# Layer b's first key and value panels planned as a pair of seven products in a two-layer trunk

## The chip, the cores and the metric

The kernel runs on one core of a Trainium2 chip. The metric is device time in microseconds (us) for one execution of the whole program, which is one launch. Engines are named as in the profile: PE (TensorE, the matmuls), PEld (its weight loads), ACT (ScalarE), DVE (VectorE), POOL (GpSimd) and SP (SyncE, which here only issues DMAs).

## The reference, cut to what matters

256 rows of 2048 numbers pass through a layer a (attention with forget gates, then an MLP with a squared ReLU) and a layer b. Between them one projection makes the keys and values that layer b attends to. All matrices are fp32.

```python
h = h + o.reshape(B, S, D) @ a_w_out[l]                      # layer a
h = h + sq_relu_mlp(h, mlp_norm_g[layer], mlp_w1[layer], mlp_w2[layer])
...
kv = rms_norm(h, kv_norm_g) @ kv_w                           # 2048 -> 4096, the panels of this case
k_sh, v_sh = jnp.split(kv, [D], axis=-1)
k_sh = rms_norm(k_sh.reshape(B, S, H, Dh), kv_k_g)           # per head
...
q = rms_norm((u @ b_w_q[l]).reshape(B, S, H, Dh), b_q_g[l])  # layer b
o = chunked_relbias_attention(q, k_sh, v_sh, b_rel[l])
h = h + o.reshape(B, S, D) @ b_w_out[l]
h = h + sq_relu_mlp(h, mlp_norm_g[layer], mlp_w1[layer], mlp_w2[layer])
```

## The kernel before, in words

**Units.** Every weight matrix is cut into panels of 512 output columns, and a panel into eight units of 128 partitions x 1024 elements: two row tiles of 128 rows each, 512 columns wide. The 256 activation rows make two blocks of 128, so a unit meets four products of 128 x 128 by 128 x 512.

**Three passes.** fp32 values are split in two. `issue` makes a weight unit's upper part with one ACT copy (L318, `hi`) and its lower part with one DVE subtraction (L319, `lo`). `passes` then runs each product three times: activation's upper part by `hi` (L585), its lower part by `hi` (L587), its upper part by `lo` (L589). A plain unit (`products`) is therefore 12 matmuls of 512 columns. Three `hi` and three `lo` buffers exist, so the split of a unit waits until the unit three places earlier has gone through its second pass (`hi`) or third pass (`lo`).

**Pairs.** Two panels that share an activation can be a `Pair`. The first two units of either panel form a 2 x 2 arrangement, `11`, `12`, `21`, `22`, and these four units are multiplied in seven smaller products in place of eight. Here the seven are called F0 to F6: `11`, T3, T2, T1, `21`, T4, `22`. T3, T2, T1 and T4 are sums of units: T3 and T2 are made by DVE (`make`, L951), T1 and T4, in most pairs, by a DMA of POOL that adds to what is there (`put`, L960). F1, F2, F3 and F6 meet sums of activations (`S`, `Sh`), made in the same manner. One such product is 6 matmuls; its results are put together by ACT copies (L985, L989, L995) and DVE operations (L990, L1002). The remaining units of both panels, a2 to a7 and b2 to b7, run plainly. In place of a unit of their own, the first four products of a pair interleave with the last three units, b5 b6 b7, of the pair before.

**Order.** The order on SP, ACT, DVE and PE is the written one. `plan_heads`, `plan_mlp` and `plan_out` write the list of units, `run` walks it. `AHEAD = 2` units are split ahead of use and `EARLY = 3` are loaded ahead of that. Other work (making the split activations `act<-y`, L410 to L414; head norms L653 to L688; attention; the steps of the hidden layer, whose sums of activations are `Sh`, L398) is cut into steps, which `run_fill` places between units. How many steps go behind each unit, and how many units after their start, stands in tables of numbers (`KM`, `HM`, `T0H`, `KX` and others); the tables with six numbers tell how many units ahead of a pair its parts `12`, `22`, `21`, `11`, T3 and T1 are loaded or made. POOL's order is the scheduler's.

**The place of the change.** At the end of layer a's MLP stand four panels of query weights, as two pairs; the last has the order `""` in `plan_mlp`. Then come keys and values: head group 0 has the panels K0 and V0, and groups 1 to 3 their own. Before the change K0 and V0 go through `panels` as plain units (16 units, the last three of V0 joined with the next pair through `Tail`), and only groups 1 to 3 are pairs, of the order `kv`. The relative-position bias is loaded by POOL ahead of each group's attention (`rel_bias`, L1214 and L1216).

Of the kernel before, what the change touches and what calls it, by code (L numbers as in the profile page):

```python
# [15 lines left out]
P = 128  # L16
# [4 lines left out]
H = 16  # L21
# [6 lines left out]
UN = 1024  # L28
AHEAD = 2
TABLES = {  # L30
    "ATA": ((11, 13, 15, 19, 9), (9, 12, 16, 18, 11), (8, 13, 15, 19, 9), (9, 9, 12, 12, 10)),
    "ATB": ((10, 13, 14, 18, 9), (9, 13, 15, 17, 11), (9, 12, 15, 17, 10), (7, 10, 12, 12, 9)),
# [13 lines left out]
    "LONG": ((0, 1, 2, 5, 9, 10, 11, 14, 14), (0, 0, 0, 4, 7, 9), (1, 0, 1, 2, 5, 5), (1, 0, 1, 4, 5, 5)),  # L46
    "OFH": (11, 10, 1, 7, 7, 7),
    "OFK": (10, 9, 4, 9, 8, 4),
# [3 lines left out]
    "OSH": (7, 9, 7, 5, 5, 1),  # L52
    "OSK": (9, 7, 4, 7, 5, 1),
    "OUTH": "F a2 a3 b2 a4 a5 b3 b4 F G F G b5 a6 a7 G b6 b7 G c2 G c3 G d2 c4 c5 G c6 c7 d3 d4",
    "OUTK": "a2 a3 F b2 a4 F b3 a5 F b4 b5 G G a6 a7 G b6 G c2 b7 d2 G c3 G c4 c5 c6 G c7 d3 d4",
    "QF": (4, 4, 2, 3, 2, 1),
    "QS": (10, 4, 4, 8, 3, 1),
    "RI": (3, 5, 7, 5),
    "SHORT": ((4, 0, 0, 3, 6, 8, 8, 9, 12), (2, 2, 3, 3, 7, 7, 8, 10, 13), (2, 0, 0, 2, 6, 7), (0, 0, 0, 2, 4, 5)),
# [39 lines left out]
def trunk(ctx: ExitStack, tc: tile.TileContext, xT, xr, gs, hg, bf, wgate, w_in, w_oa, w1a, w1fa, w1sa, w2fa, w2sa,  # L99
# [94 lines left out]
    def plan_mlp(w1, w1f, w1s, w2f, w2s, rest, when, more=None):  # L194
        pairs = []

        def add(w, wf, ws, i, wides, order, times, cols=WIDE):
            j = wides.index(i) if i in wides else i - sum(1 for k in wides if k < i)
            names = ("11", "12", "21", "22")
            if i in wides:  # L200
                m = 8 - cols // 512
                src = [[None] * (8 - m) + [ws[m * (2 * j + q) + u] for u in range(m)] for q in range(2)]
                big = {k: wf[4 * j + m] for m, k in enumerate(names)}
            else:
                src = [[w[16 * j + 8 * q + u] for u in range(8)] for q in range(2)]
                big = {k: src[int(k[1]) - 1][int(k[0]) - 1] for k in names}
            pairs.append(Pair(big, src, order, len(pairs) % 2 == 1, times, cols if i in wides else UN))

        rooms = {"12": "v0", "22": "k0", "11": "k1", "21": "v1"}
        seq = [(0, 0, 0), (0, 0, 1)]  # L210
        for c in range(NCH):
            seq += [(1, c, 0)] + [(0, c + 1, 0)] * (c + 1 < NCH) + [(1, c, 1)] + [(0, c + 1, 1)] * (c + 1 < NCH)
        for m, (second, c, q) in enumerate(seq):
            i = 2 * c + q
            if second:
                add(None, w2f, w2s, i, WIDE2, "deep%d" % q, TABLES["W2L" if i == 7 else "W2S" if q else "W2F"], DEEP)
            else:
                add(w1, w1f, w1s, i, WIDE1, "ahead%d" % q if i else "early", TABLES["W1E" + when] if not i else TABLES["W1I" + when] if i == 1 else TABLES["W1S" if q else "W1F"], DEEP)
            pairs[-1].at = second, c, q
        if more is not None:  # L220
            for q in range(2):
                add(more, None, None, q, (), "" if q else "query", TABLES["QS" if q else "QF"])
                pairs[-1].at = 1, NCH, q
        plan, rest = join(pairs, rooms, rest)
        return queue(plan + rest)

    def queue(plan):
        units.extend(Form(p, i, q == 3) if q > 1 else p.src[q][i] for p, q, i in plan)
# [28 lines left out]
                plan.append((a if t[0] in "ab" else b, "abcd".index(t[0]) % 2, int(t[1])))  # L257
        return plan, [(b, 1, u) for u in (5, 6, 7)]

    def plan_heads(w, when, w_out):  # L260
        pairs = []
        for j in range(1, w.shape[0] // 16):
            src = [[w[16 * j + 8 * q + u] for u in range(8)] for q in range(2)]
            big = {k: src[int(k[1]) - 1][int(k[0]) - 1] for k in ("11", "12", "21", "22")}
            pairs.append(Pair(big, src, "qkv" if when == "H" else "kv", j % 2 == 1, TABLES[when + ("F" if j == 1 else "S")]))
            pairs[-1].at = 2 * j
        tail = Tail(w, 8)
        units.extend(w[i] for i in range(13))
        plan, rest = join(pairs, {"12": "k0", "22": "k1", "11": "v0", "21": "v1"}, [(tail, 0, u) for u in range(KT // UA - 3, KT // UA)])
# [5 lines left out]
    plan_a = plan_mlp(w1a, w1fa, w1sa, w2fa, w2sa, rest, "H", w_qb)  # L275
    plan_k, rest, tail_k = plan_heads(w_kv, "K", w_ob)
    plan_b = plan_mlp(w1b, w1fb, w1sb, w2fb, w2sb, rest, "K")
    ready = deque()

    raws = deque()  # L280
# [420 lines left out]
    class Rooms:  # L701
# [208 lines left out]
    def bring(p, name):  # L910
# [5 lines left out]
        elif p.order in LAZY:  # L916
# [10 lines left out]
    def make(p, name, half=None):  # L927
# [89 lines left out]
    def mlp(plan, x, Sx, st, last, more=None):  # L1017
# [204 lines left out]
    def heads_b(out):  # L1222
# [135 lines left out]
```

## Time and profile before

| what | value |
|---|---|
| median of 3 runs | 2059.22 us (2059.14 to 2059.76) |
| the profiled execution | 2062.13 us, its span 2060.3 us |
| mean granted TensorE clock | 0.999 |
| PE busy | 2047.3 us, 99% |
| PEld, DVE, ACT, POOL busy | 82%, 86%, 68%, 12% |
| DMA | 556.72 MB, mean 270 GB/s |

The span is the profiled part of the execution; 1.8 us of its time lie around it. Matmuls overlap, and the ends of matmuls are modelled, so starts are read rather than ends. In the windows below the columns are PE, PEld, DVE, ACT, POOL (busy us, instructions in parentheses), granted clock (1.00 is full speed), the mean busy share of the DMA engines and GB/s.

### The profile page before, as it was taken

What the parts mean: (1) busy time and instruction counts of PE and PEld (TensorE: products, weight loads), DVE (VectorE), ACT (ScalarE), POOL (GpSimd) and SP (SyncE); (2) the same over time, 40 slices, a digit from 0 to 9 for tenths busy, and PEclk for the clock granted to TensorE, in tenths of its full rate; (3) what the DMA queues carried; (4) which work ended last, traced back from release to release, by engine and by line L of the source; (5) the groups of instructions that cost most, each with busy time, mean ns of one, the idle gap of its engine ahead of it and who ended that gap; (6) DMA issues with size and microseconds to landing.
All of it is one profiled execution on the core that took longest, in us unless ns stands there. A gap on an engine that the chain in (4) does not pass through costs nothing.

```text
span 2060.3 us, 27092 instructions
## 1 busy us (share of the span) xinstructions
PE 2047.3 (99%) x9068; PEld 1690.6 (82%) x9068; DVE 1778.3 (86%) x2058; ACT 1400.0 (68%) x1799; POOL 238.7 (12%) x347
## 2 busy tenths in 40 slices
PE   9999999999999999999999999999999999999999
PEld 8888888878888888888888888888788887888887
DVE  7788798899898899899987778888988988988996
ACT  7766566677677677677788566666766675776764
POOL 1121010011111102101012111001111111111020
PEclk9999999999999999999999999999999999999999
DMA  8898897898888898898878988889988888888985
GB/s 330 258 301 252 275 278 249 292 274 266 293 255 287 267 295 272 248 290 276 252 247 273 288 265 269 251 256 295 279 288 269 266 267 277 262 285 258 293 263 150
DMA packets 174444, 556.72 MB, mean 270 GB/s; under 512 B 40528, under 2 KB 69088, under 8 KB 151264
## 3 DMA queue, kind: packets, MB, share of 16 engines
q1 hardware_dynamic: 153824, 464.99, 63.9%
q0 software_dynamic: 20192, 89.70, 22.4%
q8 instruction: 71, 1.16, 0.2%
q14 instruction: 69, 0.57, 0.1%
q10 hardware_dynamic: 288, 0.30, 0.1%
HBM read 515.02 MB, written 27.29 MB: 263 GB/s over the span
## 4 chain that ended last, share of the span: by engine, by line
PE 88%; DMA 4%; issue 3%; DVE 3%; ACT 1%; SPq 0%; POOL 0%; ACTq 0%; DVEq 0%; POOLq 0%
PE acc L589 21%; PE acc L585 21%; PE acc L587 21%; PE s L585 8%; PE s L587 8%; PE s L589 8%; DVE lo L319 1%; DMA wT<-in_w1fb 1%; DMA q<-turn 1%; PE po L720 1%; PE po L757 1%; DMA w<-in_w2fb 1%; ACT hi L318 1%; DVE z L433 0%; DMA turn<-z 0%
## 5 line engine op out<-in xcount | busy, mean ns | idle before, releaser
L319 DVE TENSOR_TENSOR lo<-raw,hi 128x1024 fp32r<-128x1024 f32 (+1 forms) x414 | 500.3, 1213 | 81.0 <-ACT hi L318 76.6
L318 ACT ACTIVATE hi<-raw 128x1024 fp32r<-128x1024 f32 (+1 forms) x414 | 435.1, 1055 | 195.2 <-PE acc L587 128.6
L585 PE MATMUL acc<-hi,act 128*128 128x512 f32 x1784 | 500.5, 393 | 4.3 <-ACT hi L318 3.7
L589 PE MATMUL acc<-lo,act 128*128 128x512 f32 x1784 | 493.9, 390 | 0.2
L587 PE MATMUL acc<-hi,act 128*128 128x512 f32 x1784 | 493.8, 390 | 0.1
L585 PEld LDWEIGHTS acc<-hi,act 128*128 128x128 f32 x1784 | 333.1, 188 | 75.3 <-ACT hi L318 6.1
L587 PEld LDWEIGHTS acc<-hi,act 128*128 128x128 f32 x1784 | 335.1, 188 | 71.6 <-DVE act L414 1.0
L589 PEld LDWEIGHTS acc<-lo,act 128*128 128x128 f32 x1784 | 334.5, 188 | 72.4 <-DVE lo L319 3.1
L318 ACT ACTIVATE hi<-w 128x1024 fp32r<-128x1024 f32 x258 | 271.4, 1059 | 125.9 <-PE acc L587 83.5
L319 DVE TENSOR_TENSOR lo<-w,hi 128x1024 fp32r<-128x1024 f32 x258 | 310.6, 1219 | 19.6 <-ACT hi L318 17.7
L319 DVE TENSOR_TENSOR lo<-wT,hi 128x1024 fp32r<-128x1024 f32 x220 | 266.9, 1222 | 68.6 <-ACT hi L318 64.7
L318 ACT ACTIVATE hi<-wT 128x1024 fp32r<-128x1024 f32 x220 | 231.8, 1060 | 103.7 <-PE acc L587 42.2
L585 PE MATMUL s<-hi,act 128*128 128x512 f32 x530 | 146.3, 391 | 0.0
L589 PE MATMUL s<-lo,act 128*128 128x512 f32 x530 | 145.0, 389 | 0.4 <-DVE lo L319 0.4
L587 PE MATMUL s<-hi,act 128*128 128x512 f32 x530 | 144.7, 388 | 0.0
L459 POOL DMA_DIRECT2D q<-z x192 | 95.7, 511 | 250.9 <-DVE z L433 214.4
L589 PEld LDWEIGHTS s<-lo,act 128*128 128x128 f32 x530 | 99.2, 188 | 21.4 <-DVE lo L319 1.1
L587 PEld LDWEIGHTS s<-hi,act 128*128 128x128 f32 x530 | 99.4, 188 | 20.6
L585 PEld LDWEIGHTS s<-hi,act 128*128 128x128 f32 x530 | 99.2, 188 | 20.4
L585 PE MATMUL s<-hi,S 128*128 128x512 f32 x288 | 89.6, 392 | 0.0
L587 PE MATMUL s<-hi,S 128*128 128x512 f32 x288 | 88.7, 389 | 0.0
L589 PE MATMUL s<-lo,S 128*128 128x512 f32 x288 | 88.6, 389 | 0.0
(213 smaller groups left out, 2236.3 us busy)
## 6 DMA issues: line engine op xcount, KB each, us to landing
raw<-in_w_in SPq DMA_DIRECT2D x75, 512.0 KB, 5.8
w<-in_w2fa SPq DMA_DIRECT2D x32, 1024.0 KB, 6.2
w<-in_w2fb SPq DMA_DIRECT2D x32, 1024.0 KB, 6.6
w<-in_w1fa SPq DMA_DIRECT2D x28, 1024.0 KB, 7.4
w<-in_w1fb SPq DMA_DIRECT2D x28, 1024.0 KB, 7.1
raw<-in_w2sa SPq DMA_DIRECT2D x52, 512.0 KB, 7.1
raw<-in_w_kv SPq DMA_DIRECT2D x52, 512.0 KB, 5.4
raw<-in_w2sb SPq DMA_DIRECT2D x51, 512.0 KB, 7.6
```

Of the source, the lines that this page charges most:

```text
L318: S.activation(hi[:, c], raw[:, c], AF.Copy)
L319: V.tensor_tensor(lo[:, c], raw[:, c], hi[:, c].bitcast(F32), op=ALU.subtract)
L459: (G if i % 2 else SY).dma_start(dst[32 * j : 32 * j + 32, i * n : (i + 1) * n], z[32 * i : 32 * i + 32, j * n : (j + 1) * n])
L585: TE.matmul(ps[:, cols], xh, cut(hi, j), start=first, stop=False, **kw)
L587: TE.matmul(ps[:, cols], xl, cut(hi, j), start=False, stop=False, **kw)
L589: TE.matmul(ps[:, cols], xh, cut(lo, j), start=False, stop=last, **kw)
L720: TE.matmul(s[:, P : 3 * P], q[:, a, P:T], k[:, a], start=True, stop=True)
L757: TE.matmul(po[:, :T], v[:, 0, a * P : (a + 1) * P], pT[:, :2], start=True, stop=False)
```

## The change: K0 and V0 as a pair

K0 and V0 become a pair of their own, of the order `kv0`. The first two units of either panel, four plain units in all, are replaced by the seven products. F0 to F3 stand between b4 and b7 of the last query pair. For that, `12`, `22`, `21` and `11` of the new pair are loaded into the lower halves of rooms whose upper halves the last query pair now takes; T3 has a query room. `plan_mlp` hands its last three units on in place of queueing them, and `Rooms.open` takes its tile only when it is first used. The host lays out K0 like the other panels. The tables were written anew; the second W1 pair is named `second`, which has the order of units that it had before as `ahead1`.

```diff
+    "KZ": (7, 8, 3, 7, 5, 3),
-    "T0H": ((0, -1, 6, 6, 7, 7, 7, 10, 11), (1, -1, 5, 7, 7, 7, 8, 9, 9), (1, 4, 6, 6, 7, 7), (0, -1, 4, 4, 4, 5)),
+    "T0H": ((1, -1, 6, 6, 6, 6, 6, 8, 8), (0, -1, 4, 5, 6, 6, 7, 8, 8), (0, 4, 6, 7, 7, 7), (1, -1, 5, 5, 5, 5)),
...
-        return queue(plan + rest)
+        return (queue(plan), rest) if more is not None else (queue(plan + rest), [])
...
-    def plan_heads(w, when, w_out):
+    def plan_heads(w, when, w_out, rest=None):
         pairs = []
-        for j in range(1, w.shape[0] // 16):
+        for j in range(1 if rest is None else 0, w.shape[0] // 16):
...
-            pairs.append(Pair(big, src, "qkv" if when == "H" else "kv", j % 2 == 1, TABLES[when + ("F" if j == 1 else "S")]))
+            order = "qkv" if when == "H" else "kv" if j else "kv0"
+            pairs.append(Pair(big, src, order, j % 2 == 1, TABLES["KZ" if j == 0 else when + ("F" if j == 1 else "S")]))
...
-    plan_k, rest, tail_k = plan_heads(w_kv, "K", w_ob)
+    plan_k, rest, _ = plan_heads(w_kv, "K", w_ob, rest)
...
+        elif p.order == "":
+            p.t[name] = sub(p.rooms[name])[:, :UN]
...
+            elif p.order == "kv0":
+                t[name] = query_room(3)
...
-        run(plan, open_pair)
+        run(plan, open_pair, None, plan_k[0][0] if more else None)
...
-        box = [13]
-
-        def after():
-            prepare(plan_k[0][0], box[0])
-            box[0] -= 1
-
-        panels(xkv, evacs[:1], None, after)
-        panels(xkv, evacs[1:2], None, after, tail=tail_k)
...
-        "w_kv": np.concatenate([_cols_a(kv[:, :1024]), _cols_a(kv[:, 1024:], True)]),
+        "w_kv": _cols_a(kv, True),
```

Line numbers of the changed kernel are higher: L318 becomes L323, L319 L324, L398 L403, L585/L587/L589 become L590/L592/L594, L951 L962, L960 L971, L985 L996, L1214 and L1216 L1225 and L1227. On PE, at the end of the query panels, the order of before runs from the last unit of the last query pair (`s`) to the first unit of K0 (`acc`):

```order
L585 MATMUL s<-hi,act 128x512 x4
L587 MATMUL s<-hi,act 128x512 x4
L589 MATMUL s<-lo,act 128x512 x4
L585 MATMUL acc<-hi,act 128x512 x4
L587 MATMUL acc<-hi,act 128x512 x4
L589 MATMUL acc<-lo,act 128x512 x4
```

and of now, from F0 over b5 to F1, where `S` is the sums of activations:

```order
L590 MATMUL acc<-hi,act 128x512 x2
L592 MATMUL acc<-hi,act 128x512 x2
L594 MATMUL acc<-lo,act 128x512 x2
L590 MATMUL s<-hi,act 128x512 x4
L592 MATMUL s<-hi,act 128x512 x4
L594 MATMUL s<-lo,act 128x512 x4
L590 MATMUL acc<-hi,S 128x512 x2
L592 MATMUL acc<-hi,S 128x512 x2
L594 MATMUL acc<-lo,S 128x512 x2
```

F0 stands three query units earlier than K0's first unit did, and the same interleaving goes on: b6, F2, b7, F3, a2, F4, a3, a4, F5, a5, a6, a7, F6, b2. On ACT the order of now at this place holds the splits of T3 and T2 (`hi<-query`) and the copy `p<-acc`, which reads what F1 left:

```order
L323 ACTIVATE hi<-query 128x1024
L323 ACTIVATE hi<-raw 128x1024
L693 ACTIVATE q<-z,gqk 128x1024
L672 ACTIVATE qn<-acc,ss 128x128 x4
L996 ACTIVATE p_9866<-acc 128x512
L323 ACTIVATE hi<-query 128x1024
L1006 ACTIVATE acc<-acc 128x512
```

Before, the same steps of norms were followed by splits of raw units alone:

```order
L667 ACTIVATE qn<-acc,ss 128x128 x4
L318 ACTIVATE hi<-raw 128x1024
L688 ACTIVATE q<-z,gqk 128x1024
L667 ACTIVATE qn<-acc,ss 128x128 x4
L318 ACTIVATE hi<-raw 128x1024 x3
```

The copy `p<-acc` is new here and stands directly ahead of T2's split. On POOL the order of before, from the first load of the bias `rb` on, is

```order
L1214 DMA rb<-in_rel 128x4x256
L1216 MEMSET rb 64x4x64
L661 TENSOR_TENSOR ss<-ss,mhalf 128x4 x4
L960 DMA R<-in_w_kv 128x1024
L960 DMA wT_10136<-in_w_kv 128x1024
```

and of now

```order
L971 DMA R<-in_w_kv 128x1024
L666 TENSOR_TENSOR ss<-ss,mhalf 128x4 x2
L1225 DMA rb<-in_rel 128x4x256
L1227 MEMSET rb 64x4x64
L971 DMA query<-in_w_kv 128x1024
L666 TENSOR_TENSOR ss<-ss,mhalf 128x4 x2
L971 DMA R<-in_w_kv 128x1024
L971 DMA wT_10086<-in_w_kv 128x1024
```

The new pair's T1 (`R`, first row) and T4 (`query`) came in; T4 stands behind the MEMSET on `rb`. The last place is on DVE at the start of layer a's MLP, where the second set of sums `Sh` of the hidden layer is made. Before:

```order
L319 TENSOR_TENSOR lo<-raw,hi 128x1024
L319 TENSOR_TENSOR lo<-wT_4140,hi 128x1024
L951 TENSOR_TENSOR wT_4140<-wT_4140,w_4074 128x1024
L398 TENSOR_TENSOR Sh<-sum,Sh 128x512 x2
L319 TENSOR_TENSOR lo<-wT_4140,hi 128x1024
L951 TENSOR_TENSOR wT_4140<-wT_4140,w_4074 128x1024
```

and now

```order
L403 TENSOR_TENSOR Sh<-sum,Sh 128x512 x2
L324 TENSOR_TENSOR lo<-raw,hi 128x1024
L324 TENSOR_TENSOR lo<-wT_4144,hi 128x1024
L962 TENSOR_TENSOR wT_4144<-wT_4144,w_4074 128x1024
L324 TENSOR_TENSOR lo<-wT_4144,hi 128x1024
L962 TENSOR_TENSOR wT_4144<-wT_4144,w_4074 128x1024
```

The sums moved from between the two splits of `wT` to ahead of the raw unit's split.

More of the change, by code (lines that the diff above doesn't have):

```diff
@@ L30 @@
 TABLES = {
-    "ATA": ((11, 13, 15, 19, 9), (9, 12, 16, 18, 11), (8, 13, 15, 19, 9), (9, 9, 12, 12, 10)),
-    "ATB": ((10, 13, 14, 18, 9), (9, 13, 15, 17, 11), (9, 12, 15, 17, 10), (7, 10, 12, 12, 9)),
[1 row of a table removed]
+    "ATA": ((10, 13, 15, 19, 9), (9, 12, 15, 18, 12), (8, 13, 15, 19, 9), (9, 9, 12, 12, 10)),
+    "ATB": ((11, 12, 14, 18, 9), (9, 13, 15, 17, 11), (9, 12, 15, 17, 10), (7, 10, 12, 12, 10)),
[1 row of a table added]
     "GS": (1,),
[11 rows of a table removed]
-    "LONG": ((0, 1, 2, 5, 9, 10, 11, 14, 14), (0, 0, 0, 4, 7, 9), (1, 0, 1, 2, 5, 5), (1, 0, 1, 4, 5, 5)),
-    "OFH": (11, 10, 1, 7, 7, 7),
-    "OFK": (10, 9, 4, 9, 8, 4),
[3 rows of a table removed]
-    "OSH": (7, 9, 7, 5, 5, 1),
[12 rows of a table added]
+    "LONG": ((0, 1, 2, 5, 9, 10, 11, 14, 14), (0, 0, 0, 4, 7, 9), (0, 0, 1, 2, 5, 5), (1, 0, 1, 4, 5, 5)),
+    "OFH": (11, 10, 2, 7, 7, 6),
+    "OFK": (9, 9, 4, 8, 8, 4),
[3 rows of a table added]
+    "OSH": (10, 7, 9, 6, 5, 1),
     "OSK": (9, 7, 4, 7, 5, 1),
[L54 to L57, printed above, removed]
+    "OUTH": "F a2 a3 a4 b2 a5 b3 b4 F F G G b5 a6 a7 G b6 b7 G c2 G c3 G d2 c4 c5 c6 G c7 d3 d4",
+    "OUTK": "a2 a3 F b2 a4 F b3 a5 F b4 b5 G G a6 a7 G b6 G c2 b7 G d2 c3 G c4 c5 c6 G c7 d3 d4",
+    "QF": (4, 3, 2, 4, 2, 1),
+    "QS": (10, 4, 4, 8, 4, 2),
     "RI": (3, 5, 7, 5),
-    "SHORT": ((4, 0, 0, 3, 6, 8, 8, 9, 12), (2, 2, 3, 3, 7, 7, 8, 10, 13), (2, 0, 0, 2, 6, 7), (0, 0, 0, 2, 4, 5)),
[1 row of a table removed]
+    "SHORT": ((4, 0, 0, 4, 7, 7, 7, 8, 11), (2, 2, 3, 3, 7, 7, 8, 11, 13), (4, 0, 0, 2, 6, 6), (0, 0, 1, 2, 4, 5)),
[1 row of a table added]
     "T": ((1, -1, 5, 14, 14, 14, 15, 20, 20), (0, 2, 8, 10, 10, 14, 18, 20, 22), (0, -1, 5, 6, 7, 7), (0, -1, 4, 5, 5, 5)),
[4 rows of a table removed]
[4 rows of a table added]
     "W1F": (7, 5, 1, 5, 4, 3),
[2 rows of a table removed]
[2 rows of a table added]
     "W1S": (8, 6, 4, 5, 4, 1),
     "W2F": (6, 5, 1, 5, 4, 3),
[1 row of a table removed]
[1 row of a table added]
     "W2S": (7, 7, 4, 5, 3, 1),
-    "XOH": (9, 12, 13, 11),
-    "XOK": (9, 14, 12, 14),
-    "XS": (0, 5, 6, 2),
+    "XOH": (9, 13, 12, 11),
+    "XOK": (10, 14, 12, 14),
+    "XS": (0, 5, 5, 0),
 }
 EARLY = 3
-LAZY = ("qkv", "kv", "out0", "out1")
+LAZY = ("qkv", "kv", "kv0", "out0", "out1")
 UA = UN // 512
@@ L217, in plan_mlp @@
             else:
-                add(w1, w1f, w1s, i, WIDE1, "ahead%d" % q if i else "early", TABLES["W1E" + when] if not i else TABLES["W1I" + when] if i == 1 else TABLES["W1S" if q else "W1F"], DEEP)
+                add(w1, w1f, w1s, i, WIDE1, ("second" if i == 1 else "ahead%d" % q) if i else "early", TABLES["W1E" + when] if not i else TABLES["W1I" + when] if i == 1 else TABLES["W1S" if q else "W1F"], DEEP)
             pairs[-1].at = second, c, q
@@ L258, in plan_out @@
         return plan, [(b, 1, u) for u in (5, 6, 7)]
-    def plan_heads(w, when, w_out):
+    def plan_heads(w, when, w_out, rest=None):
         pairs = []
-        for j in range(1, w.shape[0] // 16):
+        for j in range(1 if rest is None else 0, w.shape[0] // 16):
             src = [[w[16 * j + 8 * q + u] for u in range(8)] for q in range(2)]
             big = {k: src[int(k[1]) - 1][int(k[0]) - 1] for k in ("11", "12", "21", "22")}
-            pairs.append(Pair(big, src, "qkv" if when == "H" else "kv", j % 2 == 1, TABLES[when + ("F" if j == 1 else "S")]))
+            order = "qkv" if when == "H" else "kv" if j else "kv0"
+            pairs.append(Pair(big, src, order, j % 2 == 1, TABLES["KZ" if j == 0 else when + ("F" if j == 1 else "S")]))
             pairs[-1].at = 2 * j
-        tail = Tail(w, 8)
-        units.extend(w[i] for i in range(13))
-        plan, rest = join(pairs, {"12": "k0", "22": "k1", "11": "v0", "21": "v1"}, [(tail, 0, u) for u in range(KT // UA - 3, KT // UA)])
+        tail = None
+        if rest is None:
+            tail = Tail(w, 8)
+            units.extend(w[i] for i in range(13))
+            rest = [(tail, 0, u) for u in range(KT // UA - 3, KT // UA)]
+        plan, rest = join(pairs, {"12": "k0", "22": "k1", "11": "v0", "21": "v1"}, rest)
         q = pairs[-1].rooms
@@ L274, in trunk @@
     plan_h, rest, tail_h = plan_heads(w_in, "H", w_oa)
-    plan_a = plan_mlp(w1a, w1fa, w1sa, w2fa, w2sa, rest, "H", w_qb)
-    plan_k, rest, tail_k = plan_heads(w_kv, "K", w_ob)
-    plan_b = plan_mlp(w1b, w1fb, w1sb, w2fb, w2sb, rest, "K")
+    plan_a, rest = plan_mlp(w1a, w1fa, w1sa, w2fa, w2sa, rest, "H", w_qb)
+    plan_k, rest, _ = plan_heads(w_kv, "K", w_ob, rest)
+    plan_b, rest = plan_mlp(w1b, w1fb, w1sb, w2fb, w2sb, rest, "K")
     ready = deque()
@@ L705, in open @@
         def open(self):
-            self.t = prob.tile([P, 4 * UN], F32, name="pbuf", tag="p", bufs=1)
+            self.t = None
             self.n = dict.fromkeys(self.at, 0)
         def __call__(self, name):
+            if self.t is None:
+                self.t = prob.tile([P, 4 * UN], F32, name="pbuf", tag="p", bufs=1)
             first, n = self.at[name]
```

44 rows, old and new, of the table TABLES are left out of this document.

## The prediction

> **What bounds the kernel now.** I read the head of the page first, then the windows by stage, then PE's waits and the chain.
>
> ```profile
> span 2060.3 us, 27092 instructions
> PE 2047.3 (99%) x9068; PEld 1690.6 (82%) x9068; DVE 1778.3 (86%) x2058; ACT 1400.0 (68%) x1799; POOL 238.7 (12%) x347
> PE 88%; DMA 4%; issue 3%; DVE 3%; ACT 1%; SPq 0%; POOL 0%; ACTq 0%; DVEq 0%; POOLq 0%
> ```
>
> PE is busy in all but 13.0 us of the span, and 88% of the chain that ended last is PE's own work. So a matmul that goes is worth its full time wherever PE is not waiting, and the rest is decided by what PE waits for. The place of the change is the stretch from 1060 to 1180 us; the other three rows are layer b's W1 start, and two windows of 11 us that stand for the starts of both MLPs.
>
> ```profile
> 1060.00:1180.00 120.00, 120.00 (x535) 99.53 (x533) 92.94 (x112) 87.43 (x139) 20.94 (x17) 1.00 0.87 269
> 1400.00:1480.00 80.00, 78.23 (x336) 63.60 (x335) 71.12 (x80) 56.34 (x67) 10.70 (x19) 0.98 0.92 296
> 455.00:466.00 11.00, 10.59 (x45) 7.93 (x44) 10.93 (x11) 7.34 (x9) 0.30 (x1) 1.00 0.97 327
> 1475.00:1486.00 11.00, 11.00 (x50) 9.10 (x49) 10.93 (x12) 8.02 (x10) 0.10 (x1) 1.00 1.04 357
> PE acc L585 <- ACT hi L318: 3.7, 4, 1.7
> PE acc L585 <- DVE acc L990: 1.9, 1, 1.9
> ```
>
> In the first row PE is busy 120.00 of 120.00 us: there is no wait to take away where K0 and V0 run, only work. The last two rows are PE's largest waits (us in all, times, longest), and neither lies in that stretch.
>
> **The matmuls.** PE's timeline around the last query unit and the first unit of K0:
>
> ```profile
> 1107.31 1.07 PE L585 MATMUL s<-hi,act 128*128 128x512 f32 x4
> 1110.03 1.07 PE L585 MATMUL s<-hi,act 128*128 128x512 f32 x4
> 1115.47 1.07 PE L585 MATMUL s<-hi,act 128*128 128x512 f32 x4
> 1118.19 1.07 PE L585 MATMUL acc<-hi,act 128*128 128x512 f32 x4
> ```
>
> These are first passes of b4, b5 and b7 of the last query pair and of K0's first unit. A unit of 12 matmuls takes 1110.03 - 1107.31 = 2.72 us, so a matmul takes 0.227 us and a product of 6 takes 1.36 us. Four plain units (48 matmuls) become seven products (42). That is 6 x 0.227 = **1.36 us less** on a PE that here never waits.
>
> **What is added on ACT and DVE.** Three more splits, T3 and T2, the combining copies and operations. The rows are groups, those of the stretch 1060 to 1180 first; two of them also give the shares of the stretch from b3 to the ninth unit of K0 and V0, and of one that is as full.
>
> ```profile
> L318 ACT ACTIVATE hi<-raw 128x1024 fp32r<-128x1024 f32 x38 | 40.1, 1063 | 14.1 <-PE acc L587 7.2 <-PE acc L589 1.7 <-DVE ss L656 1.5
> L413 ACT ACTIVATE act<-y 128x1024 fp32r<-128x1024 f32 x4 | 4.2, 1062 | 0.1
> L410 ACT ACTIVATE y<-query,gsb 128x256 f32<-128x256 f32 x8 | 3.6, 504 | 1.6 <-DVE act L414 1.6
> L653 ACT ACTIVATE sq<-acc 128x512 f32<-128x512 f32 x8 | 4.5, 592 | 3.3 <-PE acc L589 3.3
> L667 ACT ACTIVATE qn<-acc,ss 128x128 f32<-128x128 f32 x32 | 9.1, 372 | 1.6 <-POOL ss L661 1.6
> L688 ACT ACTIVATE q<-z,gqk 128x1024 f32<-128x1024 f32 x4 | 4.6, 1159 | 1.4 <-DMA z<-turn 1.4
> L985 ACT ACTIVATE p<-s 128x512 f32<-128x512 f32 x2 | 1.2, 598 | 4.5 <-PE s L589 4.5
> L319 DVE TENSOR_TENSOR lo<-raw,hi 128x1024 fp32r<-128x1024 f32 x37 | 45.0, 1222 | 9.2 <-ACT hi L318 8.8 <-PE acc L587 0.2
> L951 DVE TENSOR_TENSOR query<-query,w 128x1024 f32<-128x1024 f32 x1 | 1.2, 1226 | 0.0
> L990 DVE SCALAR_TENSOR_TENSOR acc<-s,p 128x512 f32<-128x512 f32 x2 | 1.4, 680 | 0.0
> 1085.00:1135.00 50.00, 50.00 (x223) 41.39 (x222) 36.80 (x42) 39.87 (x67) 10.96 (x8) 1.00 0.86 268
> 985.00:1010.00 25.00, 25.00 (x112) 20.71 (x111) 24.29 (x26) 18.58 (x25) 0.87 (x1) 1.00 0.87 232
> ```
>
> ACT gains 3 x 1.063 for splits and 3 x 0.598 for copies, 4.98 us: 39.87 becomes 44.9 of 50. DVE gains 3 x 1.222, 2 x 1.226 and 2 x 0.68, 7.5 us: 36.80 becomes 44.3 of 50. Both still fit, and the last row shows PE at 25.00 of 25.00 with DVE at 24.29 of 25. So none of it costs PE time by its amount; it can cost by its order.
>
> The tightest place in the order is T2's split. Now `p<-acc` stands ahead of it on ACT, and that copy waits until F1 is through. F0 takes b5's old start, 1110.03; b5 follows at 1111.39, F1 at 1114.11 and ends at 1115.47; b6 fills the time to 1118.19, where F2 needs T2's upper part, and its lower part two passes of 0.45 later, at 1119.10. After F1's end come the copy (0.60), the split's upper part (1.06) and its lower part (1.22): 1115.47 + 2.88 = 1118.35, which is 0.75 ahead of the third pass. That holds if ACT is there when F1 ends. Its queue from the split of b4 to the copy can start when the second pass of a7, three units ahead, is through (1107.31 - 3 x 2.72 + 1.81 = 1100.96). It holds five splits, two `act<-y`, six `y`, two squares, eight `qn` and one `q<-z`: 5.32 + 2.12 + 3.02 + 1.18 + 2.98 + 1.16 = 15.78 us, to 1116.7, if durations are added up. Then T2's lower part is there at 1119.6, about 0.5 us late. But starts in the trace follow each other closer than durations. An identical sequence is there for the next pair:
>
> ```profile
> 1159.19 0.60 ACT L985 ACTIVATE p<-s 128x512 f32<-128x512 f32 x1 [3.47 <-PE s L589]
> 1160.77 1.23 DVE L319 TENSOR_TENSOR lo<-wT,hi 128x1024 fp32r<-128x1024 f32 x1 [3.20 <-ACT hi L318]
> 1162.62 0.62 PE L589 MATMUL s<-lo,S 128*128 128x512 f32 x2
> ```
>
> There ACT idled 3.47 us ahead of the copy, the lower part ended at 1162.00, its pass started at 1162.62, and PE did not wait. I take **+0.2 us**, between 0 and 1.0 (twice the sum's lateness, for a DVE that is late too). Below nothing is excluded, since PE has no wait here to lose.
>
> **The sums of the hidden layer in layer a.** The tables also move work elsewhere, mostly by a place or two. One move meets a wait that the trace shows:
>
> ```profile
> 458.82 0.61 PE L585 MATMUL acc<-hi,Sh 128*128 128x512 f32 x2
> 459.44 0.73 PE L587 MATMUL acc<-hi,Sh 128*128 128x512 f32 x2
> 460.58 0.73 PE L589 MATMUL acc<-lo,Sh 128*128 128x512 f32 x2 [0.40 <-DVE lo L319]
> 461.15 1.08 PE L585 MATMUL s<-hi,act 128*128 128x512 f32 x4
> ```
>
> Three passes of 0.45 took 461.15 - 458.82 = 2.33 us in place of 1.36, because `lo` of T2's kind stood on DVE right behind `Sh`. Now `Sh` stands ahead of the raw unit's split, exactly as it stands in layer b, before and after. Layer b's window (1475 to 1486) has PE at 11.00 of 11.00 us. So I take **-0.97 us**; the ends are -0.97 and 0, the latter if another split is late for it.
>
> The other moves of tables I cost at 0, since the same work lies on the same engines a place or two away, under a PE that is busy 99%. The bound is the largest single wait of PE above, 1.9 us, either way.
>
> **The sum.** -1.36 + 0.2 - 0.97 = -2.13. The profiled execution took 2062.13 us (its span 2060.3, and 1.83 around it), so it would take 2060.0. The median of the runs stands 2.91 below the profiled execution; by the same distance the forecast is **2057.1 us**. Against the median that is -0.1%; a measurement of this kernel can tell apart from no change about 0.2%, which is 4.1 us.
>
> **The clock.** One wait of layer b's W1 start costs more than itself:
>
> ```profile
> 1441.43 12.97 DMA wT<-in_w1fb
> 1454.50 1.06 ACT hi L318
> 1455.00:1460.00 5.00, 4.39 (x12) 3.52 (x13) 4.41 (x4) 3.72 (x5) 0.18 (x1) 0.66 0.80 304
> ```
>
> An accumulating DMA landed after 12.97 us, PE waited for the split behind it (the 1.7 us wait for `hi` above), and in the next 5 us the granted clock was 0.66: 5 x 0.34 = 1.7 us lost. So a stall of this size, not its bare length, is the price of a late T4: up to twice as much. The Trainium skill, page "TensorE: Matmul & The Clock Gate", section "Part 1: The HAM clock gate", says that the clock halves after an idle window of about 3.4 us, and that pauses of PE beyond that are to be avoided. By that rule a new wait of under 3.4 us in the new pair would not slow the clock, and the sum's ends would be 1.7 us closer; the trace does not agree, as 1.7 us of waiting were enough here, and I keep the trace's price. In layer b's MLP I leave wait and clock as they are, since POOL's order there is the same.
>
> **The rivals.** *Waits go too.* Thirteen us of PE's span are not busy, and the rewritten tables move parts of pairs in both MLPs. If the late T4 at 1454 lands in time, 1.7 us of waiting and 1.7 us of clock go with it: -2.13 - 3.4 = -5.5, **2053.7 us**. Against it: that DMA's row on POOL is unmoved and the queues are as full. Chance 0.17.
>
> *The new pair eats its gain.* If ACT and DVE queue up from F1 to F6, at most one buffer's lateness of about 1 us at T2 and again behind T1 (each the bound above), the total is about -0.1 to 0: with `Sh` not helping either, **2059.1 us**. For it: 44.9 and 44.3 of 50 us, with waits on both sides. Against it: the full window at 985 us. Chance 0.16.
>
> *T4 is late behind the bias.* This one ends slower. T4 of the new pair is an accumulating DMA, and on POOL it stands behind the MEMSET on `rb`, which waits for the landing of `rb`; PE needs T4 at F5.
>
> ```profile
> 1113.21 0.83 POOL L1214 DMA_DIRECT2D rb<-in_rel  x1 [1.00 <-DVE act L414]
> 1119.28 0.30 POOL L1216 MEMSET rb<- 64x256 f32 x1 [5.24 <-DMA rb<-in_rel]
> DMA to landing us min/median/max: 5.0/5.9/8.2
> DMA to landing us min/median/max: 5.2/9.3/13.0
> ```
>
> The last two rows are the landings of L1214 (the bias) and of L960 (all accumulating DMAs). F5 is due at 1110.03 + 5 x 1.36 + 6 x 2.72 = 1133.15 (five products and six plain units stand ahead), so T4 must have landed by 1132.1, one split earlier. With the issue at 1113.21 and the medians it lands at 1113.21 + 0.83 + 5.9 + 0.30 + 9.3 = 1129.5, in time by 2.6 us. With the longest of both, and 2.4 us of new DVE work ahead of what `rb` waits for (T3's sum and a split, 1.226 + 1.222), it lands at 1138.0, 5.9 us late, and the clock's 1.7 us come on top: -2.13 + 5.9 + 1.7 = +5.5, **2064.7 us**. It decides against the change when T4 lands later than 1132.1 + 0.4, and past the 0.2% when later than about 1136.6. Chance 0.08, since both longest landings must meet.
>
> That the change does not do what it says I leave out: the order shows F0 to F3 among the query units, and 42 matmuls for 48.
>
> **How the numbers follow.** The forecast, 0.59, lies between -3.3 (without the T2 lateness, and with 1.0 us more found by the tables) and about 0, that is 2055.9 to 2059.2. The chances of the rivals are 0.17, 0.16 and 0.08. Faster by over 0.2% (under 2055.1): the first rival, 0.17, and 0.03 of the forecast's tail: 0.20. Slower by over 0.2% (over 2063.3): T4's worst landings, 0.08, of which some end within, and an unseen wait with the halved clock (1.9 + 1.7 on top of a lost gain, about 2062.8): together 0.08. Within: 0.72. The range that leaves 2 in 10 out reaches to the first rival's 2053.7 and above to 2061.5 (the lost gain, 2059.1, with one such wait of 1.9 and a little more).
>
> **What would show it.** Right: PE's timeline has F0 at the place of b5, seven products of 1.36 us, no PE wait between b4 and b2 of the new pair, F5 about 23 us behind F0; the three passes with `Sh` in layer a's MLP start take 1.36 us; ACT's `p<-acc` starts within 1 us of F1's end. Wrong: the accumulating `query<-in_w_kv` lands after F5's time and PE waits on ACT `hi` there; a granted clock below 1.00 in the pair's window; or waits that come or go in windows that this text costs at 0, above all at 1454 us.

## The result, and the profile after

The changed kernel took 2055.78 us (median of 22 runs, 2053.41 to 2059.09) against 2059.63 us before (22 runs beside them, 2056.45 to 2063.48): a ratio of 0.9982, 95% interval 0.9976 to 0.9988. That is 3.8 us faster, just inside the 0.2% that the prediction called no change and inside its range, with nearly double the movement that it forecast (2.1 us). One kernel's runs differ by several us, so sizes below rest on ratios and on traces, not on single times.

The head of the page of the changed kernel, with PE's two largest waits (us, times, longest):

```profile
span 2053.8 us, 27091 instructions
PE 2044.1 (100%) x9062; PEld 1688.7 (82%) x9062; DVE 1784.0 (87%) x2065; ACT 1403.6 (68%) x1805; POOL 244.3 (12%) x349
PE 97%; DVE 2%; ACT 1%; issue 1%; DMA 0%; ACTq 0%; DVEq 0%
PE acc L594 <- DVE lo L324: 2.4, 2, 1.4
PE s L594 <- DVE lo L324: 1.3, 1, 1.3
```

PE's share of the chain rose from 88% to 97%; DMA, 4% before, left it. The waits for ACT's `hi` behind a late DMA and for `acc L990` are gone from the top, and waits for `lo` have come in their place. By stage, the windows that answer to those of before:

```profile
1060.00:1180.00 120.00, 118.71 (x524) 97.48 (x523) 97.63 (x116) 90.88 (x145) 24.41 (x19) 1.00 0.89 275
1105.00:1140.00 35.00, 35.00 (x156) 28.99 (x155) 29.51 (x33) 28.69 (x47) 9.59 (x7) 1.00 0.97 288
1085.00:1135.00 50.00, 50.00 (x222) 41.38 (x222) 43.29 (x50) 43.31 (x72) 14.35 (x10) 1.00 0.98 304
1400.00:1480.00 80.00, 79.93 (x350) 64.91 (x348) 74.04 (x82) 58.46 (x71) 10.70 (x19) 1.00 0.94 297
```

Where the new pair runs (second row) PE is busy all the time. The first row has a new wait of 1.3 us, ahead of the pair. Layer b's W1 start (last row) lost its wait and its slow clock in this trace. PE's timeline at the pair (first passes of b4, F0, b5 and F2, the third pass of F2, and the first of F5):

```profile
1108.40 1.07 PE L590 MATMUL s<-hi,act 128*128 128x512 f32 x4
1111.12 0.62 PE L590 MATMUL acc<-hi,act 128*128 128x512 f32 x2
1112.48 1.07 PE L590 MATMUL s<-hi,act 128*128 128x512 f32 x4
1119.28 0.62 PE L590 MATMUL acc<-hi,S 128*128 128x512 f32 x2
1120.19 0.62 PE L594 MATMUL acc<-lo,S 128*128 128x512 f32 x2
1134.24 0.62 PE L590 MATMUL acc<-hi,act 128*128 128x512 f32 x2
```

A product takes 1.36 us, a unit 2.72, and F5 comes 23.12 us behind F0, as worked out. It is 23.12 us in the traces of all eight runs that have the pair and one load of the bias.

### The profile page after: what moved, and what is told of

It is laid out like the page before. It is cut to its first block, busy times and chain, and to the rows that moved or that the text cites. A ratio compares the mean times of both kernels' runs of the same rounds, so it can differ in the third digit from the quotient of the medians.

```text
span 2053.8 us, 27091 instructions
## 1 busy us (share of the span) xinstructions
PE 2044.1 (100%) x9062; PEld 1688.7 (82%) x9062; DVE 1784.0 (87%) x2065; ACT 1403.6 (68%) x1805; POOL 244.3 (12%) x349
## 4 chain that ended last, share of the span: by engine, by line
PE 97%; DVE 2%; ACT 1%; issue 1%; DMA 0%; ACTq 0%; DVEq 0%
PE acc L594 22%; PE acc L590 22%; PE acc L592 22%; PE s L590 9%; PE s L594 9%; PE s L592 9%; DVE lo L324 1%; PE po L727 1%; PE po L764 1%; PE po L765 0%; PE po L726 0%; ACT hi L323 0%; DMA raw<-in_w_in 0%; PE pg L866 0%; DVE act L1045 0%
## 5 line engine op out<-in xcount | busy, mean ns | idle before, releaser
L324 DVE TENSOR_TENSOR lo<-raw,hi 128x1024 fp32r<-128x1024 f32 (+1 forms) x409 | 493.9, 1212 | 82.7 <-ACT hi L323 78.2
L323 ACT ACTIVATE hi<-raw 128x1024 fp32r<-128x1024 f32 (+1 forms) x409 | 429.3, 1054 | 191.8 <-PE acc L592 132.6
L590 PE MATMUL acc<-hi,act 128*128 128x512 f32 x1774 | 496.9, 393 | 1.0 <-ACT hi L323 0.8
L594 PE MATMUL acc<-lo,act 128*128 128x512 f32 x1774 | 491.4, 390 | 1.5 <-DVE lo L324 1.4
L592 PE MATMUL acc<-hi,act 128*128 128x512 f32 x1774 | 490.7, 389 | 0.0
L594 PEld LDWEIGHTS acc<-lo,act 128*128 128x128 f32 x1774 | 332.1, 188 | 73.7 <-DVE lo L324 4.8
L592 PEld LDWEIGHTS acc<-hi,act 128*128 128x128 f32 x1774 | 332.8, 188 | 70.3 <-DVE act L381 0.5
L590 PEld LDWEIGHTS acc<-hi,act 128*128 128x128 f32 x1774 | 331.3, 188 | 70.4 <-ACT hi L323 2.3
L323 ACT ACTIVATE hi<-w 128x1024 fp32r<-128x1024 f32 x254 | 267.2, 1058 | 123.6 <-PE acc L592 83.7
L324 DVE TENSOR_TENSOR lo<-wT,hi 128x1024 fp32r<-128x1024 f32 x220 | 267.1, 1221 | 65.6 <-ACT hi L323 61.8
L324 DVE TENSOR_TENSOR lo<-w,hi 128x1024 fp32r<-128x1024 f32 x254 | 305.4, 1217 | 14.2 <-ACT hi L323 12.6
L323 ACT ACTIVATE hi<-wT 128x1024 fp32r<-128x1024 f32 x220 | 232.1, 1060 | 102.7 <-PE acc L592 50.4
L590 PE MATMUL s<-hi,act 128*128 128x512 f32 x530 | 146.3, 391 | 0.0
L594 PE MATMUL s<-lo,act 128*128 128x512 f32 x530 | 145.2, 389 | 0.0
L592 PE MATMUL s<-hi,act 128*128 128x512 f32 x530 | 144.8, 388 | 0.0
L594 PEld LDWEIGHTS s<-lo,act 128*128 128x128 f32 x530 | 99.0, 188 | 21.6 <-DVE lo L324 1.3
L592 PEld LDWEIGHTS s<-hi,act 128*128 128x128 f32 x530 | 99.3, 188 | 20.7
L590 PEld LDWEIGHTS s<-hi,act 128*128 128x128 f32 x530 | 99.1, 188 | 20.2
L594 PE MATMUL s<-lo,S 128*128 128x512 f32 x288 | 88.8, 390 | 1.3 <-DVE lo L324 1.3
L590 PE MATMUL s<-hi,S 128*128 128x512 f32 x288 | 89.4, 392 | 0.0
L592 PE MATMUL s<-hi,S 128*128 128x512 f32 x288 | 88.7, 389 | 0.0
```

The lines of the kernel that those rows point to most:

```text
L323: S.activation(hi[:, c], raw[:, c], AF.Copy)
L324: V.tensor_tensor(lo[:, c], raw[:, c], hi[:, c].bitcast(F32), op=ALU.subtract)
L590: TE.matmul(ps[:, cols], xh, cut(hi, j), start=first, stop=False, **kw)
L592: TE.matmul(ps[:, cols], xl, cut(hi, j), start=False, stop=False, **kw)
L594: TE.matmul(ps[:, cols], xh, cut(lo, j), start=False, stop=last, **kw)
```

## The experiments

The runs of every experiment are set against runs of the kernel before on the same chip. In some of these kernels line numbers stand 6 lower or so than in the changed kernel.

**Both kernels again.** No edit.

> The kernel before once more, for a second trace. If the two long waits of its first trace (1.9 us at 1454 us behind the late accumulating DMA of W1, 2.1 us at 1734 us behind a late load of W2) belong to the order of the program, both are here again at 1.5 to 2.5 us each, and so is the wait of about 1 us at the second set of sums of layer a (459 us). If they are chance of DMA landings, at least one of the two is gone or moved, while the one at 459 us, which is DVE's order, stays within 0.2 us.

> The changed kernel once more. Ratio to before 0.9982 within 0.001. The waits that are DVE's order stay: 1.2 us at 1032 us and 1.4 us at 1072 us (T3 of the last query pair waits for its unit R). If the T3 wait hangs on how late R lands, it moves by more than 0.5 us. Between 1105 and 1140 us PE has no wait in either case.

The kernel before, once more, took 2059.47 us; its span was 2057.6 us. Two windows of its second trace, at 459 us and at 1734 us:

```profile
455.00:466.00 11.00, 10.59 (x45) 7.98 (x44) 10.93 (x12) 7.38 (x10) 0.55 (x1) 1.00 0.95 328
1728.00:1738.00 10.00, 10.00 (x45) 8.27 (x45) 8.54 (x9) 8.19 (x9) 0.87 (x1) 1.00 1.04 320
```

The wait at 459 us is there again, since it is DVE's order. The one at 1734 us is not, and the one at 1454 us was smaller. So part of the 6.5 us between the first two spans is chance of DMA landings. The changed kernel again: 0.9983 (0.9975 to 0.9992), with the wait at 1072 us at 0.80 us between starts in place of 1.45 (what the starts of two matmuls stand apart beyond the usual 0.227); the one at 1032 us stayed at 1.2, and from 1105 to 1140 us PE again had none.

**The pair alone, and the tables alone.**

```diff
 # pair_alone: the changed kernel with before's tables, except KM, KX, KZ, ORD, FO
 # tables_alone: the kernel before with the changed tables, except KM, KX, ORD, FO
```

> K0 and V0 as a pair, with all tables of before but those that the pair itself needs (KM, KX, KZ and the order of its units). Theory of the prediction: 6 matmuls less and nothing else, -1.4 us (with up to 1.0 us given back), the wait at 459 us is still there at 1.0 us. Rival, the tables carry the rest: the same -1.4 us or less here, and the other 2 us only with the tables. Rival, the pair alone costs more than it saves at T2 or T4: 0 or slower, with a PE wait between 1105 and 1140 us.

> The kernel before with the changed kernel's tables for everything but K0 and V0 (KM, KX and the orders stay as before). Theory of the prediction: -0.97 us, from 459 us alone. Rival, the tables carry the rest: -2.3 us, with the wait at 1454 us below 0.6 us and full clock there. Rival, what is won in layer a is handed back: the lead over before is 1 to 2 us at 500 us, and below 1 us at 1050 us, as DVE and not PE sets the pace from 985 to 1035 us.

The pair alone: 0.9981 (0.9973 to 0.9990). The tables alone: 0.9994 (0.9984 to 1.0003), which can't be told from nothing. The pair by itself carries the whole effect, 3.9 us with an interval of 2.1 to 5.6. That is more than the 1.4 us expected, which lies outside the interval: six matmuls explain 1.36 of it and leave the rest open. The rival that the tables carry the rest fell, as the pair has it without them. In the trace of the tables alone the wait at 459 us is gone, which their time does not show. In the trace of the pair alone it is still there, and PE had no wait from 1085 to 1180 us:

```profile
1085.00:1180.00 95.00, 95.00 (x423) 78.76 (x422) 76.24 (x90) 71.88 (x111) 19.64 (x15) 1.00 0.96 295
```

**The turn of the raw buffers.** Every fifth raw load of an MLP goes to the buffer `zraw`, by a counter of all raw loads. K0 and V0 as a pair need four raw loads fewer, so in layer b's MLP it is another fifth. The counter was shifted at that MLP's start: in the kernel before, by one, to have the changed kernel's turn; in the changed kernel, by four, to have the old one.

```diff
         base, extra[0] = turns[0], True
+        extra[1] += 1 if more is None else 0     # before_phase; 4 in after_phase
```

> The kernel before, with one edit: the counter of raw loads goes one on when layer b's MLP starts. Every fifth raw load of an MLP goes to a buffer of its own (zraw); K0 and V0 as a pair take four raw loads away ahead of that MLP, so the changed kernel has another fifth. With this edit the kernel before has the changed kernel's. No matmul goes. Theory that this phase carries what the six matmuls do not explain: -1.5 to -2.5 us, no wait of 2 us at 1734 us, the last-but-one accumulating DMA of W1 (at 1935 us) landing after 8.5 to 9 us in place of 11.3, and no wait near 1949 us. Rival, chance: 0 within 0.8 us, and that landing stays above 11.

> The changed kernel with the counter set four on at the same place, so that layer b's MLP has the zraw buffers of the kernel before. If the phase carries 1.5 to 2.5 us, this one is only 1.2 to 2 us faster than before (ratio 0.9990 to 0.9994), and the landing at 1935 us is above 11 us again, with 0.5 to 0.8 us of PE waits behind it. If it is chance, the ratio is that of the changed kernel, 0.998.

Measured: 0.9993 (0.9984 to 1.0003) for the kernel before with the new turn, 0.9988 (0.9979 to 0.9997) for the changed kernel with the old turn. Neither time is settled by itself. The traces are clear. The accumulating DMA of W1 at 1935 us, its landing, and the 16 us around the wait behind it, for the kernel before and for it with the new turn:

```profile
1937.19 0.86 POOL L960 DMA_DIRECT2D wT<-in_w1fb  x1 [18.93 <-DVE Sh L398]
DMA to landing us min/median/max: 11.2/11.2/11.2
1940.00:1956.00 16.00, 15.82 (x69) 12.42 (x68) 14.67 (x19) 9.36 (x10) 0.00 (x0) 1.00 0.94 290
```

```profile
1937.47 0.86 POOL L960 DMA_DIRECT2D wT<-in_w1fb  x1 [18.60 <-DVE Sh L398]
DMA to landing us min/median/max: 8.2/8.2/8.2
1940.00:1956.00 16.00, 16.00 (x72) 13.22 (x71) 15.97 (x20) 10.21 (x11) 0.00 (x0) 1.00 0.93 296
```

PE got 72 matmuls through in place of 69: three of 0.227 us, 0.7 us. The landing follows the turn and not the pair: 11.2 us again in the changed kernel with the old turn, 8.5 in the changed kernel. So about 0.7 us of the gain comes from there, which the expectation had put at 1.5 to 2.5. The wait of 2 us at 1734 us, which was to go as well, is not in the trace with the new turn, but neither is it in the second trace of the kernel before.

**T0H added to the pair alone.**

```diff
 # pair_t0h: pair_alone with the changed kernel's T0H
```

> K0 and V0 as a pair, the tables that they need, and of all other new tables T0H alone (the sums Sh of both MLP starts' kind in layer a). Theory of the prediction: 0.97 us faster than the pair alone, as the wait at 459 us goes. Rival: what is won at 459 us is handed back where the late accumulating DMA of W2 (12 us in the pair's traces, 10.7 before) sets the pace at 1007 us; then the lead over the pair alone is 1 us at 500 us and 0 at 1050 us.

0.9983 (0.9974 to 0.9991), not to be told from the pair alone by time. In the trace the second set of sums went as forecast. The three passes with `Sh` and the pass behind them, in the pair alone and with T0H:

```profile
457.58 0.61 PE L584 MATMUL acc<-hi,Sh 128*128 128x512 f32 x2
458.20 0.73 PE L586 MATMUL acc<-hi,Sh 128*128 128x512 f32 x2
459.33 0.74 PE L588 MATMUL acc<-lo,Sh 128*128 128x512 f32 x2 [0.40 <-DVE lo L318]
459.91 1.09 PE L584 MATMUL s<-hi,act 128*128 128x512 f32 x4
```

```profile
458.99 0.61 PE L584 MATMUL acc<-hi,Sh 128*128 128x512 f32 x2
459.44 0.61 PE L586 MATMUL acc<-hi,Sh 128*128 128x512 f32 x2
459.96 0.74 PE L588 MATMUL acc<-lo,Sh 128*128 128x512 f32 x2
460.54 1.09 PE L584 MATMUL s<-hi,act 128*128 128x512 f32 x4
```

2.33 us became 1.55: 0.78 us won there. Counted between the same matmuls at 450 and 480 us, 0.43 us of it are left, as PE's next passes are later by little waits; in the other traces with the new T0H it is 0.2 to 0.9. The rival, that this is handed back at 1007 us, was half right: something is lost there, but with the pair, T0H or not. The last accumulating DMA of layer a's W2 and ACT's wait for it, before and in the changed kernel, with PE's wait 27 us on:

```profile
DMA to landing us min/median/max: 10.6/10.6/10.6
1007.11 2.15 ACT L318 ACTIVATE hi<-wT 128x1024 fp32r<-128x1024 f32 x2 [1.02 <-DMA wT<-in_w2fa]
1034.40 0.73 PE L589 MATMUL acc<-lo,S 128*128 128x512 f32 x2 [0.41 <-DVE lo L319]
```

```profile
DMA to landing us min/median/max: 12.0/12.0/12.0
1006.47 2.01 ACT L323 ACTIVATE hi<-wT 128x1024 fp32r<-128x1024 f32 x2 [2.35 <-DMA wT<-in_w2fa]
1033.74 0.73 PE L594 MATMUL acc<-lo,S 128*128 128x512 f32 x2 [1.05 <-DVE lo L324]
```

In the four traces without the pair this DMA landed after 10.6 to 11.5 us, in the nine with it after 10.6 to 12.6, in seven of them after 11.6 or more. Where it is late, PE waits 0.6 us longer for `lo` at 1034 us: between starts, 0.55 to 0.67 us after landings of 10.6 to 10.8 us and 1.06 to 1.23 after 11.1 to 12.6, in all thirteen traces, with the pair or not. In the tables alone, which have T0H and no pair, it landed after 10.7 us. Why it lands later with the pair is open: the loads of SP and POOL ahead of it are the same, in the same order.

**T3 of the last query pair.** The changed kernel's DVE stood at T3's sum until its unit, just loaded, had landed:

```profile
1063.53 1.23 DVE L962 TENSOR_TENSOR query<-R 128x1024 f32<-128x1024 f32 x1 [3.13 <-DMA R<-in_w_qb]
1073.65 0.73 PE L594 MATMUL s<-lo,S 128*128 128x512 f32 x2 [1.29 <-DVE lo L324]
```

The old row of the table makes T3 (and T1) one unit later, so that one more split stands ahead of the sum, 1.14 us between starts, and the unit has that much longer to land.

```diff
-    "QS": (10, 4, 4, 8, 4, 2),
+    "QS": (10, 4, 4, 8, 3, 1),
```

> The changed kernel with one table row of before: the last query pair makes T3 three units ahead of its start and not four, and T1 one ahead and not two. In the changed kernel's trace DVE stood 3.1 us at T3's sum for the unit R that had just been loaded, and PE lost 1.4 us at 1072 us. Theory: that wait falls below 0.4 us, and the time by 1.0 to 1.5 us against the changed kernel (ratio to before 0.9976). Rival: PE is only let run into the next late thing, T4 of the new pair or DVE at 1110 us, and the time stays.

> The changed kernel once more, to stand beside the next one on the same chip. Ratio to before 0.998 within 0.001; PE waits between 0.3 and 1.5 us at 1072 us.

> The changed kernel with the old row QS for the last query pair, once more, to tell it from the changed kernel. Theory: 1 us faster than that (T3's sum no longer stands in DVE's queue ahead of its load). Rival: the same within 0.5 us, as the wait at 1072 us changed from run to run (1.4 and 0.8 us so far) and something else follows.

The two runs of the edit gave 0.9977 (0.9967 to 0.9986) and 0.9978 (0.9968 to 0.9988); the changed kernel in its third run 0.9983 (0.9974 to 0.9992). On the same chip that was 2056.33 against 2057.81 us, 1.5 us. The intervals overlap, so the times do not settle it. The place, from 1060 to 1105 us in the first trace of the changed kernel and in the second with the edit:

```profile
1060.00:1105.00 45.00, 43.71 (x192) 35.66 (x191) 38.81 (x46) 36.72 (x61) 9.43 (x7) 1.00 0.81 260
```

```profile
1063.69 1.23 DVE L956 TENSOR_TENSOR query<-R 128x1024 f32<-128x1024 f32 x1 [1.73 <-DMA R<-in_w_qb]
1060.00:1105.00 45.00, 45.00 (x199) 36.83 (x198) 39.63 (x47) 37.47 (x63) 9.44 (x7) 1.00 0.84 268
```

Here DVE still waits, 1.73 us in place of 3.13, and PE does not. In the first trace with the edit DVE waited 2.08 us and PE lost 0.41 between starts. What PE loses follows DVE's wait for that load and not the row alone. With the new row DVE waited 3.13, 2.91, 2.48, 2.42 and 1.76 us in five traces, and PE lost 1.45, 1.23, 0.80, 0.74 and 0.07: each time 1.7 us less. The 2.08 and 0.41 of the old row show the same difference. In the pair alone, and with T0H added, DVE waited 0.88 and 0.47 us and PE lost nothing. No later wait came in place of this one up to F5, which was the rival. By its ratios this is the fastest version that was run.

**The bias loaded twice.** It doubles what stands ahead of the new pair's T4 on POOL.

```diff
         G.dma_start(rb[:, :, :T], src)
+        if g == 0:
+            G.dma_start(rb[:, :, :T], src)
```

> The changed kernel with the load of the bias issued twice for the first head group (same bytes, same place). It doubles what stands ahead of T4 of the new pair on POOL. In the changed kernel T4 is issued at 1119.95 us, lands after 9.5 us at 1129.45, and PE takes F5 at 1134.24, its split 1.06 us earlier at the latest: 3.7 us to spare. The second load waits until the first has landed (5 us or more), so T4 lands at about 1135. Theory of the slower rival in the prediction: PE waits 1.5 to 3 us at F5, and the time grows by that, to 3 us more if the clock halves; ratio to before 0.999 to 1.0005. If POOL has more room than I see, there is no wait at F5 and the ratio stays at 0.998.

0.9997 (0.9988 to 1.0006): the gain is gone, some 2.9 us against the other runs of the changed kernel by the ratios, 3.7 by the medians of the runs beside each other (2061.50 and 2057.81). T4 in the changed kernel, and with the second load (there ACT's and PE's waits for it too, and a wait of DVE behind them):

```profile
1118.11 0.30 POOL L1227 MEMSET rb<- 64x256 f32 x1 [4.71 <-DMA rb<-in_rel]
1119.95 0.88 POOL L971 DMA_DIRECT2D query<-in_w_kv  x1 [1.55 <-DVE lo L324]
DMA to landing us min/median/max: 9.5/9.5/9.5
```

```profile
1122.63 0.31 POOL L1229 MEMSET rb<- 64x256 f32 x1 [5.90 <-DMA rb<-in_rel]
1123.28 0.91 POOL L971 DMA_DIRECT2D query<-in_w_kv  x1 [0.34 <-DVE lo L324]
1132.57 1.06 ACT L323 ACTIVATE hi<-query 128x1024 fp32r<-128x1024 f32 x1 [5.57 <-DMA query<-in_w_kv]
1133.68 0.73 PE L590 MATMUL acc<-hi,act 128*128 128x512 f32 x2 [1.38 <-ACT hi L323]
1145.13 1.22 DVE L962 TENSOR_TENSOR wT<-R 128x1024 f32<-128x1024 f32 x1 [4.20 <-DMA R<-in_w_kv]
1105.00:1180.00 75.00, 72.86 (x317) 58.32 (x316) 55.43 (x64) 50.74 (x79) 14.72 (x12) 1.00 0.92 283
```

In the changed kernel the MEMSET was no bound: T4 waited 1.55 us more, for T2's `lo`. With the second load T4 came late and PE waited 1.4 us at F5. The rest followed behind it: ACT's splits and SP's loads came later too, DVE stood 4.20 us at the next pair's T3 for its load (3.58 in the changed kernel), and PE waited 0.5 us more at 1147 us for the `lo` behind that. From 1105 to 1180 us 317 matmuls went through in place of 333 in the changed kernel, 16 x 0.227 = 3.6 us. The clock stayed at 1.00.

## Why the prediction was right, and where it was short

The time came inside the range. The six matmuls are the part of the sum that was right; the rest of the agreement is partly luck. Losses at 1034 and 1072 us, which the sum left out, took back about what its term for `Sh` won, and the gain beyond the matmuls came from places that it had put at nothing.

- **The matmuls.** Right. Six matmuls went, and PE has no wait from 1105 to 1140 us, so all of 1.36 us counts.
- **T2's split, +0.2.** It cost nothing. ACT waited for F1 and not the other way, and the lower part was there in time:

```profile
1116.76 0.60 ACT L996 ACTIVATE p<-acc 128x512 f32<-128x512 f32 x1 [1.02 <-PE acc L594]
1118.34 1.23 DVE L324 TENSOR_TENSOR lo<-query,hi 128x1024 fp32r<-128x1024 f32 x1 [1.33 <-ACT hi L323]
```

  It ended at 1119.57, 0.62 us ahead of the third pass at 1120.19; 0.75 had been worked out from F1's end. Adding up ACT's durations (15.8 us) was the wrong upper end: from the start of the first split at 1102.26 to the end of the last norm at 1115.74 the same work took 13.5 us, and ACT then idled 1.02 us.
- **The sums Sh, -0.97.** The mechanism is right, the size at most 0.8 us: 2.33 us became 1.54 to 1.59 in the nine traces with the new T0H, and part of that went again by 480 us. In the times it does not show, as the changed kernel takes as long as the pair alone; the wait for T3 of the last query pair can take as much away.
- **The other moves at 0.** This step failed. At 1072 us, where neither the kernel before nor the pair alone waits, the changed kernel lost 1.45, 0.80 and 1.23 us in its three traces. The prediction quoted ACT's and DVE's order around the pair, but did not follow T3's sum and the load of its unit onto the same place of the table (both four units ahead in QS), where DVE stands until the landing. The row QS alone does not set the loss: with the old row PE still lost 0.41 us in one trace of two, and with the new row only 0.07 in one of five, by how late the unit landed.
- **Layer b's MLP as before.** This failed too. Taking four raw loads away changed the turn of `zraw`, though not POOL's order, and with it one landing by 2.7 us and PE by about 0.7 us.
- **Waits go too.** This rival half came: the wait at 1454 us and its slow clock are not in this trace. But in the pair alone that wait was 1.9 us, so it varies from run to run and is no sure gain of the order. The wait at 1734 us, which came and went as well, goes with the landing of another accumulating DMA, of W2 (12.3 us before, 8.6 after): over the thirteen traces PE lost 2.1 us or more there after 12.2 and 12.3 us, 1.6 after 11.6, and at most 0.9 after 10.6 or less.
- **The pair eats its gain.** It did not happen. ACT and DVE reached 43.3 of 50 us each, near the 44.9 and 44.3 forecast, and PE lost nothing. The price of this rival does not follow from its terms: two waits of 1.0 us against 1.36 us of matmuls make +0.6, not -0.1 to 0.
- **T4 behind the bias.** It did not happen, and the second load showed that it is how the change would have been lost. Its own margin was 3.7 us: landed at 1129.45, split due at 1133.18. That 1129.5 had been worked out from the medians is luck. The path through the bias left out that T4 adds to T2's tile and so waits for T2's `lo`; the bias came 1.8 us sooner than the sum had it (MEMSET at 1118.11 and not 1119.94), and the wait for `lo` took 1.55 us.

What stays open: of the pair's 3.9 us (2.1 to 5.6), matmuls make 1.36 and the turn of `zraw` 0.7, while the DMA of layer a's W2, mostly later with the pair, takes about 0.6 back. Part of the rest can be read from the granted clocks. Of the kernel before's 87 runs beside the experiments, 27 have a mean clock under 1.000; of the 99 runs of the kernels with the pair and one load of the bias, 11. In the traces a mean of 0.999 is one stretch at a lower clock, 1.7 us lost, and the kernel before's 27 runs took 2.3 us longer than its others beside them. So an estimate from these numbers is (0.31 - 0.11) x 2.3 = 0.5 us: with the pair PE is less often held up long enough. Why is not shown. What remains, 1.3 us and what W2 takes back, is of the size of the waits that vary from run to run at 1454 and 1734 us, and these few traces can't say how often each kernel meets them.

## What to carry to other kernels

A step that is costed at nothing because only its number in a table moves still has to be followed to its load: an in-order engine that reaches a sum before its operand has landed holds up all that is behind it. A change that removes loads also moves every rotation that counts loads, and so what competes with transfers hundreds of us later. Where a DMA is the last term of a chain, double what stands ahead of it: that shows its margin and its price in one run.

## What the runs showed of the hardware

How long an accumulating DMA takes to land can hang on what runs beside it: the one at 1935 us took 11.2 to 11.4 us in all four traces with the old turn, 8.2 to 8.8 us in all nine with the new. Others vary by chance: in three traces of the same changed kernel the one of W2 at 1718 to 1721 us took 8.6, 10.5 and 10.6 us.

The granted clock fell after waits of about 2 us, but not always: after four of the six waits of 1.9 to 2.4 us between starts. In the tables alone PE waited 2.0 us at 1732 us (first row), and the next window shows the granted clock at 0.66; in the changed kernel's third trace it waited 1.8 us at 275 us, and the clock is 0.83 in the window around it.

```profile
PE acc L579 <- DVE acc L984: 2.0, 1, 2.0
1735.00:1740.00 5.00, 5.00 (x17) 3.96 (x16) 4.39 (x6) 2.11 (x2) 0.00 (x0) 0.66 0.98 289
```

```profile
PE s L590 <- ACT hi L323: 1.8, 1, 1.8
275.00:280.00 5.00, 3.19 (x10) 2.19 (x10) 3.89 (x6) 4.25 (x8) 1.39 (x2) 0.83 0.99 380
```

In the pair alone PE was held up as long at 1453 us, and the clock stayed:

```profile
PE acc L584 <- ACT hi L317: 3.8, 4, 1.9
1455.00:1460.00 5.00, 4.83 (x20) 3.67 (x21) 4.91 (x5) 3.97 (x5) 0.00 (x0) 1.00 0.70 249
```

No wait of 1.6 us or less between starts was followed by a lower clock in any trace. The prediction's price of 1.7 us for a wait of this size is therefore an upper one: four times in six is 1.1 us on average.
